# Recurrent layer of a bidirectional encoder: TensorE's order written out by hand, small products grouped, recurrence and within-chunk products given new places in two periods

## The chip, the cores and the metric

The kernel runs on one core of one Trainium2 chip. The metric is the device time of one launch in microseconds (us); the time before is the median of three runs, 2247.12 us (2247.01 to 2252.69).

## The reference

Two residual layers over 256 tokens of width 2048, and a last RMS norm. Layer 1 (a gated MLP with a spatial gate) is not touched. Layer 0 is an RWKV-7 mixer with 64 heads of 64, scanned in both directions:

```python
z = h @ w_in                                  # 2048 -> r, k, v, gate (4096 each), low-rank dw, da
zs = zs + mu_prev * (shift_prev(zs) - zs) + mu_next * (shift_next(zs) - zs)
for d, rev in ((0, False), (1, True)):
    decay = exp(-exp(-softplus(-(w0[d] + tanh(dw[:, :, d]) @ w_up[d])) - 0.5))
    a_d = sigmoid(a0[d] + da[:, :, d] @ a_up[d])
    k_d = k * (1.0 + (a_d - 1.0) * k_a)
    # S_t = S_{t-1} diag(w_t) + (S_{t-1} a_t) b_t^T + v_t k_t^T ;  y_t = S_t r_t
    y = y + wkv_scan(rh, decay, k_d, vh, -kk, kk * a_d, rev)      # kk: k * k_k, normed per head
    bonus = bonus + sum(rh * k_d * r_k) * vh
out = group_norm(y) * ln_w + ln_b + bonus
return (out * silu(gate)) @ w_out
```

## The kernel before, in words

Products in fp32 precision are made of three products of halves: each weight tile is loaded to `raw` (SP's queue, two buffers), ScalarE (ACT) rounds it to its high half `whi`, VectorE (DVE) subtracts to get the low half `wlo`, and `mm3` issues high x high, low x high, high x low on TensorE (PE). A weight tile has four of 16 rows of blocks: `whi_wv7_12` is the last quarter of block 7's v weights.

The 64 heads are worked in 16 blocks of 4 heads (NB = 16). A loop over periods p = 0 to 17 pipelines them. In period p `mains` makes the wide projections of 128x256 (`acck`, `accr` of block p, `accv`, `accg` of block p-1: 384 matmuls); `factors(p)` makes decays and scaled keys (`hs_k`, `hb_k`: sums over heads; `up`: low-rank products into the bank "pf"; `TH`, `TA`: their tanh; `AR`, `BK`: scaled factors); `before(p-1)` makes the within-chunk products `gp` (grams; masked into `Gs` by DVE) for both directions d and then `inverses` (`Dt`, `NQ`: copies of Gs by ACT; `La`, a chain of 31 pairs of DVE steps on `X` and `TD`; `Tn`, `qp`); `transposed_factors` makes `bp` and `BT`; `after(p-2)` makes `values` (`vp`, copied into `SUV` by ACT, and `RC`), the recurrence over four chunks i (`chain`: `xp`, copied to `Xs`; `uu`, copied to `SUV`; `sp`, from which DVE makes the next state `SJ` and ACT copies it to `SUV`; `yp`), and `finish` (group norm, `bb`, `yt`, output). In names, gp7_011 is block 7, half of the heads 0, direction 1, column tile 1; xp6_1 is block 6, chunk 1.

Each of these is a generator that yields times t within a period of 78; a small loop runs whichever is due next. That gives the order in which instructions are emitted. A scheduler then sets the order of every engine's queue with a timeline of its own, in which the emitted order is the priority; an instruction that would wait in this timeline is passed by others. Semaphores between engines follow the final order, and each queue executes strictly in it.

Of the kernel before, what the change touches and what calls it, by code (L numbers as in the profile page):

```python
# [22 lines left out]
def trunk(tc, x, norm_g, final_norm_g, w_in, mu_prev, mu_next, w0, w_up, a0, a_up, k_k, k_a, r_k,  # L23
# [438 lines left out]
    def factors(b, f):  # L462

        cts = (2 * b, 2 * b + 1)
        t0 = 4 * MT + 1
        yield t0
        Kt = f["Kt"]

        SQ = fr.tile([P, 2, T], F32, tag="SS", name=f"SQ{b}")
        for cl in range(2):  # L470
            S.activation(SQ[:, cl], Kt[:, cl], AF.Square, scale=nkkc[:, cts[cl]:cts[cl] + 1])
# [1 line left out]
        n2 = fr.tile([P, TT, 4], F32, tag="n2", name=f"n2_{b}")
        V.tensor_scalar(n2, head_sums(SQ, f"hs_k{b}"), 1e-24, None, ALU.max)
        rn = fr.tile([P, TT, 4], F32, tag="rn", name=f"rn{b}")
        G.tensor_tensor(rn.rearrange("p a b -> p (a b)"), n2.rearrange("p a b -> p (a b)"), halfpow, ALU.pow)
        yield t0 + 8
        rnb = head_bcast(rn, f"hb_k{b}", "pf", 1, fr.tile([P, TT, 4, 64], F32, tag="SS", name=f"exk{b}"))
        yield t0 + 12
        NK = fr.tile([P, 2, T], F32, tag="NK", name=f"NK{b}")  # L480
# [4 lines left out]
        AR = sc.tile([P, 2, 2, NC, 2, C], F32, tag="AR", name=f"AR{b}", bufs=2)  # L485
        yield TUP
        _, wh, wl = f["wu"]
        ups = []
# [73 lines left out]
        f.update(PA=PA, AR=AR, BK=BK, BQ=BQ)  # L562

    def grams(b, f):

# [1 line left out]
        Gs = sc.tile([P, 2, 16, 2 * C], F32, tag="Gs", name=f"Gs{b}", bufs=2)
        for d in range(2):
            for cl in range(2):

                gp = [sm(f"gp{b}_{h}{d}{cl}").rearrange("p (c q t) -> p c q t", c=NC, q=2) for h in range(2)]
                for c in range(NC):
                    for h in range(2):
                        PE.matmul(gp[h][:, c].rearrange("p q t -> p (q t)"),  # L574
                                  BK[H[h], d, cl, c].rearrange("p q t -> p (q t)"),
                                  AR[H[h], d, cl, c].rearrange("p q t -> p (q t)"), start=True, stop=True)
                u0 = (d * 2 + cl) * NC
                for h in range(2):
                    V.tensor_tensor(Gs[:, h, u0:u0 + NC], gp[h].rearrange("p c q t -> p c (q t)"),
                                    gmask[:, d].rearrange("p q t -> p (q t)").unsqueeze(1).to_broadcast([P, NC, 2 * C]),  # L580
                                    ALU.mult)
                yield 4 * (d * 2 + cl + 1)
        f["Gs"] = Gs

# [14 lines left out]
    def inverses(b, f):  # L599
# [8 lines left out]
        for h in range(2):  # L608
# [3 lines left out]
            S.copy(NQ[h * 64:h * 64 + 32], Gs[0:32, h, :, 32:64])  # L612
# [10 lines left out]
        for j in range(31, 0, -1):  # L623
            yield TSUB - (TSUB - 21) * j / 31
            m, n = j // 2, 16 - j // 2
            tv = TD[:, :j * n].rearrange("p (s t) -> p s t", t=n)
            V.tensor_tensor(tv, La[:, j, 0:j].unsqueeze(2).to_broadcast([P, j, n]),  # L627
                            X[:, j:j + 1, m:].to_broadcast([P, j, n]), ALU.mult)
            V.tensor_tensor(X[:, 0:j, m:], X[:, 0:j, m:], tv, ALU.add)  # L629
# [24 lines left out]
    def values(b, f):  # L654

        Vt = f["Vt"]
        SUV = sc.tile([P, 2, 2, NC, 2, C], F32, tag="SUV", name=f"SUV{b}")
        G.memset(SUV[H[0], :, :, 0].rearrange("p d l h v -> p (d l) (h v)"), 0.0)
        vp = sm(f"vp{b}", "pq", 1).rearrange("p (m n) -> p m n", n=P)
        yield 4  # L660
        for cl in range(2):
            for tt in range(TT):
                PE.transpose(vp[:, cl * TT + tt], Vt[:, cl, tt * P:(tt + 1) * P], ident)
        for d in range(2):

            rows_ = SUV[H[1], d].rearrange("p l c h n -> p (l c) (h n)")
            if d == 1:
                rows_ = rows_[:, ::-1]
            for half in range(2):
                S.copy(rows_[:, half::2], vp[H[half]])  # L670
        for h in range(2):
            S.copy(RC[H[0], h], f["AR"][H[h], :, :, :, 1].rearrange("p d l c t -> p (d l c) t"))
# [487 lines left out]
```

## Time and profile before

| | |
|---|---|
| median of three runs | 2247.12 us |
| profiled execution, its own time | 2250.88 us |
| its span | 2249.2 us, mean granted TensorE clock 0.991 |
| busy: PE, PEld, DVE, ACT, POOL | 98%, 87%, 72%, 63%, 8% |
| periods 0 to 5 (from the first `acck` to that of block 6) | 37.9 to 473.4 us |
| periods 6 to 15 | 473.4 to 1265.7 us |
| periods 16 and 17 and the rest of layer 0 | from 1265.7 us |
| layer 1 and the end | about 1430 to 2249 us |

Span is the time from the first to the last instruction; busy time counts an engine's instructions and not its waits. A busy TensorE can still be slowed by what stands next to what in its queue, which shows in the distance of starts and not in the busy share.

### The profile page before, as it was taken

How to read it: one execution, taken by the hardware profiler on the slowest of the kernel's cores; microseconds unless marked ns; L12 is line 12 of the kernel's file. 1: busy time of each engine (PE TensorE's matmuls, PEld its weight loads, DVE VectorE, ACT ScalarE, POOL GpSimd, SP SyncE). 2: the span in 40 equal slices, each digit the busy share in tenths (PEclk: the TensorE clock that was granted, in tenths of full speed). 3: DMA queues.
4: the chain of work that ended last, by engine and by line, in shares of the span. 5: the costliest groups of instructions: out<-in, count | busy, mean ns of one | idle time of the engine just before them, and what ended most of it. 6: DMA issues, size and time to landing. Idle time of an engine off the chain costs nothing.

```text
span 2249.2 us, 48589 instructions
## 1 busy us (share of the span) xinstructions
PE 2200.9 (98%) x19984; PEld 1959.1 (87%) x19984; DVE 1611.2 (72%) x3121; ACT 1406.3 (63%) x2192; POOL 181.0 (8%) x230
## 2 busy tenths in 40 slices
PE   7999999999999999999999999999999999999998
PEld 7898899999999999999999977778888888888886
DVE  5787789778877977877887774465546777777444
ACT  6657777777767777776777864455444444444443
POOL 2210101001011101101010000000000000000000
PEclk9999899999999999999999999999999999999999
DMA  5444244343343343334434455586776666666664
GB/s 169 132 129 132 69 116 116 105 119 114 113 126 109 111 116 119 115 112 125 118 102 125 128 174 175 186 259 189 207 221 192 194 195 193 194 192 194 196 195 156
DMA packets 286127, 339.23 MB, mean 151 GB/s; under 512 B 11600, under 2 KB 233552, under 8 KB 285776
## 3 DMA queue, kind: packets, MB, share of 16 engines
q1 hardware_dynamic: 265648, 314.88, 46.4%
q10 hardware_dynamic: 20256, 21.24, 3.2%
q8 instruction: 157, 2.57, 0.5%
q14 instruction: 66, 0.54, 0.1%
HBM read 329.78 MB, written 6.29 MB: 149 GB/s over the span
## 4 chain that ended last, share of the span: by engine, by line
PE 76%; ACT 10%; DMA 6%; DVE 5%; issue 3%; POOL 0%; ACTq 0%; POOLq 0%; SPq 0%; DVEq 0%
PE uacc L200 5%; PE gacc L200 5%; PE oacc L162 4%; PE oacc L161 4%; PE oacc L163 4%; PE gp L574 4%; PE gacc L202 3%; PE uacc L202 3%; PE vacc L161 3%; PE vacc L162 3%; PE vacc L163 3%; PE accv L161 3%; PE accg L161 2%; PE accg L163 2%; PE accg L162 2%
## 5 line engine op out<-in xcount | busy, mean ns | idle before, releaser
L200 PE MATMUL uacc<-z,whi_u 128*128 128x512 f32 x512 | 179.0, 394 | 0.0
L200 PE MATMUL gacc<-z,whi_g 128*128 128x512 f32 x512 | 177.3, 393 | 0.0
L161 PE MATMUL accv<-zh,whi_wv 128*128 128x256 f32 x512 | 153.9, 301 | 2.3 <-ACT whi_wv L146 2.3
L163 PE MATMUL accg<-zh,wlo_wg 128*128 128x256 f32 x512 | 151.3, 295 | 0.5 <-DVE wlo_wg L147 0.5
L161 PE MATMUL acck<-zh,whi_wk 128*128 128x256 f32 x512 | 150.3, 294 | 1.1 <-ACT whi_wk L146 1.1
L163 PE MATMUL acck<-zh,wlo_wk 128*128 128x256 f32 x512 | 148.6, 290 | 2.7 <-DVE wlo_wk L147 2.7
L163 PE MATMUL accv<-zh,wlo_wv 128*128 128x256 f32 x512 | 149.7, 292 | 1.6 <-DVE wlo_wv L147 1.5
L163 PE MATMUL accr<-zh,wlo_wr 128*128 128x256 f32 x512 | 149.3, 292 | 0.5 <-DVE wlo_wr L147 0.4
L162 PE MATMUL accr<-zl,whi_wr 128*128 128x256 f32 x512 | 148.5, 290 | 0.0
L161 PE MATMUL accr<-zh,whi_wr 128*128 128x256 f32 x512 | 148.3, 290 | 0.0
L161 PE MATMUL accg<-zh,whi_wg 128*128 128x256 f32 x512 | 148.0, 289 | 0.0
L162 PE MATMUL accv<-zl,whi_wv 128*128 128x256 f32 x512 | 147.6, 288 | 0.0
L162 PE MATMUL acck<-zl,whi_wk 128*128 128x256 f32 x512 | 147.3, 288 | 0.0
L162 PE MATMUL accg<-zl,whi_wg 128*128 128x256 f32 x512 | 146.4, 286 | 0.0
L202 PE MATMUL uacc<-z,wlo_u 128*128 128x256 f32 x512 | 142.4, 284 | 0.0
L202 PE MATMUL gacc<-z,wlo_g 128*128 128x256 f32 x512 | 140.2, 279 | 0.0
L147 DVE TENSOR_TENSOR wlo_v<-raw_v,whi_v 128x1024 fp32r<-128x1024 f32 x64 | 78.4, 1225 | 80.3 <-ACT whi_v L146 80.3
L627 DVE TENSOR_TENSOR TD<-La,X 128x126 f32<-128x126 f32 (+22 forms) x496 | 126.7, 255 | 10.5
L629 DVE TENSOR_TENSOR X<-X,TD 128x126 f32<-128x126 f32 (+22 forms) x496 | 125.0, 252 | 9.4
L147 DVE TENSOR_TENSOR wlo_o<-raw_o,whi_o 128x1024 fp32r<-128x1024 f32 x64 | 78.0, 1223 | 74.6 <-ACT whi_o L146 74.3
L147 DVE TENSOR_TENSOR wlo_p<-raw_p,whi_p 128x1024 fp32r<-128x1024 f32 x60 | 73.9, 1232 | 75.6 <-ACT whi_p L146 75.6
L146 ACT CAST whi_p<-raw_p 128x1024 fp32r<-128x1024 f32 x60 | 63.1, 1051 | 91.5 <-PE oacc L163 87.3
(333 smaller groups left out, 6946.9 us busy)
## 6 DMA issues: line engine op xcount, KB each, us to landing
raw_wk<-in_rwkv_w_in_dram SPq DMA_DIRECT2D x64, 512.0 KB, 3.8
raw_wr<-in_rwkv_w_in_dram SPq DMA_DIRECT2D x64, 512.0 KB, 3.7
raw_wv<-in_rwkv_w_in_dram SPq DMA_DIRECT2D x64, 512.0 KB, 3.8
raw_wg<-in_rwkv_w_in_dram SPq DMA_DIRECT2D x64, 512.0 KB, 3.7
raw_o<-in_rwkv_w_out_dram SPq DMA_DIRECT2D x64, 512.0 KB, 4.0
raw_v<-in_gmlp_w_in_dram SPq DMA_DIRECT2D x64, 512.0 KB, 3.7
raw_u<-in_gmlp_w_in_dram SPq DMA_DIRECT2D x64, 512.0 KB, 3.5
raw_g<-in_gmlp_w_in_dram SPq DMA_DIRECT2D x64, 512.0 KB, 3.5
```

The costliest lines, as they stand in the source:

```text
L146: latest[0] = S.copy(hi, raw)
L147: latest[1] = V.tensor_tensor(lo, raw, hi.bitcast(F32), ALU.subtract)
L161: PE.matmul(acc, a[0], b[0], start=first, stop=False, skip_group_check=True)
L162: PE.matmul(acc, a[0], b[1], start=False, stop=False, skip_group_check=True)
L163: PE.matmul(acc, a[1], b[0], start=False, stop=last, skip_group_check=True)
L200: PE.matmul(acc.rearrange("p h t -> p (h t)"), hi[:, j, cs], zc[:, k].rearrange("p h t -> p (h t)"), start=k == 0, stop=False, skip_group_ ...
L202: PE.matmul(acc[:, 0], lo[:, j, cs], zc[:, k, 0], start=False, stop=k == KT - 1, skip_group_check=True)
L574: PE.matmul(gp[h][:, c].rearrange("p q t -> p (q t)"), BK[H[h], d, cl, c].rearrange("p q t -> p (q t)"), AR[H[h], d, cl, c].rearrange("p q ...
L627: V.tensor_tensor(tv, La[:, j, 0:j].unsqueeze(2).to_broadcast([P, j, n]), X[:, j:j + 1, m:].to_broadcast([P, j, n]), ALU.mult)
L629: V.tensor_tensor(X[:, 0:j, m:], X[:, 0:j, m:], tv, ALU.add)
```

## The change

TensorE's queue in the loop over periods is no longer ordered by the scheduler: it executes in the emitted order (`tc.manual_schedule(engines={PE})`). The other engines' queues are still ordered by the scheduler. The emission times are set anew:

- the recurrence starts at 2 (before: 9) with a distance of 13 between chunks (11), `uu` and `sp` 3.5 and 7.6 after `xp` (3.0 and 5.9);
- grams of direction 0 are made at 59.1 and 66.1 in the period of their factors, those of direction 1 at 2.1 and 5.6 in the next one (all four: 0 to 12 of the next period);
- the inverse's steps are spread from 8 to 44 (18 to 50), its products `qp` stand at 59 and 66 (53 and 55);
- `values` moves from 4 in period p to 72 in period p-1;
- the low-rank products leave `factors` for `rates`, at 40, 43, 46, 50 (43 and on, 2 apart); `hs_k` stands at 28.8 (22.5), `hb_k` at 35 (28.5); the factors' steps move by some units;
- `yt` stands at 66 (60), and `OT` has a buffer of its own.

The core of the diff:

```diff
-    PERIOD, CT, TSUB, TBT, TEO, TUP = 78.0, 11.0, 50.0, 36.0, 1.2, 43.0
+    PERIOD, CT, TBT, TEO = 78.0, 13.0, 37.0, 1.2
+    TCH, CB, TUP = 2.0, (3.5, 7.6), (40.0, 43.0, 46.0, 50.0)
+    TGP, TSUB, TQ, TYT = ((59.1, 66.1), (TCH + 0.1, TCH + CB[0] + 0.1)), (8.0, 44.0), (59.05, 66.0), 66.05
...
+    def rates(b, f):
+        f["ups"] = [[], []]
+        for d in range(2):
...
+            for wi, (dst, hb) in enumerate(((th, hw0), (ta, ha0))):
+                yield TUP[2 * d + wi]
+                up = sm(f"up{b}_{d}_{wi}", "pf", 1).rearrange("p (c t) -> p c t", c=2)
...
-        yield t0 + 2
+        yield 28.8
         n2 = fr.tile([P, TT, 4], F32, tag="n2", name=f"n2_{b}")
...
-    def grams(b, f):
+    def grams(b, f, d):
...
+        for cl in range(2):
+            yield TGP[d][cl]
             gp = [sm(f"gp{b}_{h}{d}{cl}").rearrange("p (c q t) -> p c q t", c=NC, q=2) for h in range(2)]
...
+    def early_grams(b, f):
+        yield TGP[0][0]
+        yield from grams(b, f, 0)
...
-            yield TSUB - (TSUB - 21) * j / 31
+            yield TSUB[1] - (TSUB[1] - TSUB[0] - 2) * j / 31
...
     def values(b, f):
+        yield 72
...
-            t = 9 + CT * i
+            t = TCH + CT * i
...
-        OT = sc.tile([P, 2, T], F32, tag="vy", name=f"OT{b}", bufs=2)
+        OT = sc.tile([P, 2, T], F32, tag="OT", name=f"OT{b}")
...
     def before(b, f):
-        yield from grams(b, f)
+        yield from grams(b, f, 1)
         yield from inverses(b, f)
     def after(b, f):
-        yield from values(b, f)
         yield from chain(b, f)
...
+    fixed = tc.manual_schedule(engines={mybir.EngineType.PE})
+    fixed.__enter__()
     for p in range(NB + 2):
...
-            act.append(factors(p, st[p]))
+            act += [rates(p, st[p]), factors(p, st[p]), early_grams(p, st[p])]
         if 0 < p <= NB:
-            act += [before(p - 1, st[p - 1]), transposed_factors(p - 1, st[p - 1])]
+            act += [before(p - 1, st[p - 1]), values(p - 1, st[p - 1]), transposed_factors(p - 1, st[p - 1])]
...
+    fixed.__exit__(None, None, None)
```

In period 0 the emitted order also puts all four `up` and the first two pairs of grams of block 0 ahead of block 1's `acck`.

What moves is seen best at three places of period 8. First TensorE where chunk 0 of block 6's recurrence begins (`xp6_0`), beside block 8's k projection (`acck8`) and the grams of block 7. The queue before:

```order
L163 MATMUL acck8_8396<-zh_187,wlo_wk8_4_8363 128x256
L574 MATMUL gp7_110_8498<-AR7_7755,BK7_8114 128x128
L574 MATMUL gp7_010_8497<-AR7_7755,BK7_8114 128x128
L574 MATMUL gp7_110_8498<-AR7_7755,BK7_8114 128x128
L161 MATMUL acck8_8396<-zh_187,whi_wk8_8_8399 128x256
L162 MATMUL acck8_8396<-zl_188,whi_wk8_8_8399 128x256
L701 MATMUL xp6_0_8521<-SUV6_8428,Gs6_7311 64x64 x2
L163 MATMUL acck8_8396<-zh_187,wlo_wk8_8_8400 128x256
L161 MATMUL acck8_8396<-zh_187,whi_wk8_8_8399 128x256
L162 MATMUL acck8_8396<-zl_188,whi_wk8_8_8399 128x256
L163 MATMUL acck8_8396<-zh_187,wlo_wk8_8_8400 128x256
L701 MATMUL xp6_0_8521<-SUV6_8428,Gs6_7311 64x64 x6
```

Three of gp7's grams stand in one piece and xp6_0 in two, with one to four wide matmuls between. TensorE's queue at the same xp6_0 after the change (left out are five more grams, alternating the same way):

```order
L167 MATMUL acck8_8436<-zh_187,wlo_wk8_0_8354 128x256
L713 MATMUL xp6_0_8465<-SUV6_8402,Gs6_7120 64x64 x8
L584 MATMUL gp7_010_8476<-AR7_7868,BK7_8081 128x128
L584 MATMUL gp7_110_8477<-AR7_7868,BK7_8081 128x128
...
L584 MATMUL gp7_110_8477<-AR7_7868,BK7_8081 128x128
L165 MATMUL acck8_8436<-zh_187,whi_wk8_0_8353 128x256
```

The grams and xp6_0 stood in pieces of two to six matmuls between wide ones; now xp6_0's eight and the eight grams of one pair stand in one group. The next pair follows `uu6_0` in the same way, 18 wide matmuls later.

Second ACT between the copy of xp6_0 and the copy of the next state into SUV, which xp6_1 on TensorE reads. ACT's queue before:

```order
L706 COPY Xs6_0_8530<-xp6_0_8521 128x256
L611 COPY Dt7_8618<-Gs7_8415 32x16x32 x2
L612 COPY NQ7_8619<-Gs7_8415 32x512
L712 COPY SUV6_8428<-uu6_0_8544 64x4x64 x2
L611 COPY Dt7_8618<-Gs7_8415 32x16x32 x2
L146 CAST whi_wr8_4_8575<-raw_wr8_4_8573 128x1024
L612 COPY NQ7_8619<-Gs7_8415 32x512
L621 COPY Gs7_8415<-AR7_7755 64x16x64
L146 CAST whi_wr8_8_8650<-raw_wr8_8_8648 128x1024
L391 ACTIVATE kt8_8640<-acck8_8396,c0_174 128x256
L621 COPY Gs7_8415<-AR7_7755 64x16x64
L729 COPY SUV6_8428<-SJ6_0_8608 64x4x64 x2
```

ACT's queue between the same two copies after the change:

```order
L718 COPY Xs6_0_8474<-xp6_0_8465 128x256
L150 CAST whi_wk8_12_8496<-raw_wk8_12_8494 128x1024
L724 COPY SUV6_8402<-uu6_0_8512 64x4x64 x2
L623 COPY Dt7_8535<-Gs7_8224 32x16x32 x2
L624 COPY NQ7_8536<-Gs7_8224 32x512
L623 COPY Dt7_8535<-Gs7_8224 32x16x32 x2
L624 COPY NQ7_8536<-Gs7_8224 32x512
L150 CAST whi_wr8_0_8565<-raw_wr8_0_8563 128x1024
L633 COPY Gs7_8224<-AR7_7868 64x16x64
L741 COPY SUV6_8402<-SJ6_0_8592 64x4x64 x2
L633 COPY Gs7_8224<-AR7_7868 64x16x64
L150 CAST whi_wr8_4_8624<-raw_wr8_4_8622 128x1024
```

The same copies of Gs stand there, but uu6_0's copy is ahead of them now, only one cast instead of two and no `kt` stand among them; the state's copy SUV<-SJ6_0 comes after one Gs<-AR and not after two. The grams that they read are made right behind uu6_0 now.

Third DVE near the end of the inverse of block 7, where it makes the low half of the last quarter of the v weights, `wlo_wv7_12`. DVE's queue before:

```order
L627 TENSOR_TENSOR TD7_8639<-La7_8632,X7_8634 128x96
L629 TENSOR_TENSOR X7_8634<-X7_8634,TD7_8639 128x8x12
L627 TENSOR_TENSOR TD7_8639<-La7_8632,X7_8634 128x91
L147 TENSOR_TENSOR wlo_wv7_12_9036<-raw_wv7_12_9033,whi_wv7_12_9035 128x1024
L629 TENSOR_TENSOR X7_8634<-X7_8634,TD7_8639 128x7x13
L627 TENSOR_TENSOR TD7_8639<-La7_8632,X7_8634 128x78
L536 TENSOR_TENSOR TH8_0_9045<-TH8_0_9045,kt8_8640 128x512
L539 SCALAR_TENSOR_TENSOR TA8_0_9046<-TA8_0_9046,NK8_8855 128x512
```

DVE's queue around the same wlo_wv7_12 after the change:

```order
L641 TENSOR_TENSOR X7_8557<-X7_8557,TD7_8562 128x16
L644 STREAM_TRANSPOSE TD7_8562<-X7_8557 128x32x16
L542 TENSOR_TENSOR TH8_0_8455<-TH8_0_8455,kt8_8679 128x512
L645 STREAM_TRANSPOSE Tn7_9089<-TD7_8562 128x512
L545 SCALAR_TENSOR_TENSOR TA8_0_8456<-TA8_0_8456,NK8_8968 128x512
L556 TENSOR_TENSOR BK8_9185<-TH8_0_8455,SS8_0_9126 128x8x64
L754 BN_STATS st6_6_9202<-yp6_8457 128x6 x8
L151 TENSOR_TENSOR wlo_wv7_12_9061<-raw_wv7_12_9058,whi_wv7_12_9060 128x1024
L555 TENSOR_TENSOR BK8_9185<-TA8_0_8456,SS8_0_9126 128x8x64
L755 BN_AGGR mv6_9203<-st6_6_9202 128x2 x8
```

The low half stood among the steps on X; now it comes behind the last of them, both transposes, two of block 8's factors, BK and the group norm's statistics of block 6 (`st6_6`).

More of the change, by code (lines that the diff above doesn't have):

```diff
@@ L460, in mains @@
                 yield 12 * MT + i
[L462 to L471, printed above, removed]
-        yield t0 + 2
[L473 to L480, printed above, removed]
-        for cl in range(2):
-            V.scalar_tensor_tensor(NK[:, cl], Kt[:, cl], nkkc[:, cts[cl]:cts[cl] + 1], rnb[:, cl], ALU.mult, ALU.mult)
-        PA = sc.tile([P, NC, 2, 2], F32, tag="PA", name=f"PA{b}", bufs=3)
[L485 to L488, printed above, removed]
+    def rates(b, f):
+        f["ups"] = [[], []]
         for d in range(2):
@@ L498, in factors @@
                 for cl in range(2):
-                    S.activation(dst[:, cl], up[:, cl], AF.Tanh, scale=0.5, bias=hb[d][:, cts[cl]:cts[cl] + 1])
-                yield TUP + 2 * (2 * d + wi + 1)
-            ups.append((th, ta))
+                    S.activation(dst[:, cl], up[:, cl], AF.Tanh, scale=0.5, bias=hb[d][:, 2 * b + cl:2 * b + cl + 1])
+                f["ups"][d].append(dst)
+    def factors(b, f):
+        cts = (2 * b, 2 * b + 1)
+        yield 4 * MT + 1
+        Kt = f["Kt"]
+        SQ = fr.tile([P, 2, T], F32, tag="SS", name=f"SQ{b}")
+        for cl in range(2):
+            S.activation(SQ[:, cl], Kt[:, cl], AF.Square, scale=nkkc[:, cts[cl]:cts[cl] + 1])
+        yield 28.8
+        n2 = fr.tile([P, TT, 4], F32, tag="n2", name=f"n2_{b}")
+        V.tensor_scalar(n2, head_sums(SQ, f"hs_k{b}"), 1e-24, None, ALU.max)
+        rn = fr.tile([P, TT, 4], F32, tag="rn", name=f"rn{b}")
+        G.tensor_tensor(rn.rearrange("p a b -> p (a b)"), n2.rearrange("p a b -> p (a b)"), halfpow, ALU.pow)
+        yield 35
+        rnb = head_bcast(rn, f"hb_k{b}", "pf", 1, fr.tile([P, TT, 4, 64], F32, tag="SS", name=f"exk{b}"))
+        yield 38
+        NK = fr.tile([P, 2, T], F32, tag="NK", name=f"NK{b}")
+        for cl in range(2):
+            V.scalar_tensor_tensor(NK[:, cl], Kt[:, cl], nkkc[:, cts[cl]:cts[cl] + 1], rnb[:, cl], ALU.mult, ALU.mult)
+        PA = sc.tile([P, NC, 2, 2], F32, tag="PA", name=f"PA{b}", bufs=3)
+        AR = sc.tile([P, 2, 2, NC, 2, C], F32, tag="AR", name=f"AR{b}", bufs=2)
+        f.update(PA=PA, AR=AR)
         KD = []
@@ L504, in factors @@
         for d in range(2):
-            t = (TUP + 4, PERIOD * 0.7)[d]
+            t = (46, 55)[d]
             yield t
-            th, ta = ups[d]
+            th, ta = f["ups"][d]
             S.activation(th, th, AF.Identity, bias=1.0)
@@ L536, in factors @@
             eng.tensor_tensor(th, th, Kt, ALU.mult)
-            yield t + 6
+            yield t + 5
             V.scalar_tensor_tensor(ta, ta, 1.0, NK, ALU.add, ALU.mult)
             if d == 0:
-                yield PERIOD * 0.6
+                yield 52
                 BK = se.tile([P, 2, 2, NC, 2, C], F32, tag="BK", name=f"BK{b}")
+                f["BK"] = BK
             def slot(q, natural):
@@ L554, in factors @@
             KD.append(th)
+        yield 67
         eng.tensor_tensor(KD[0], KD[0], KD[1], ALU.add)
-        yield PERIOD * 0.94
+        yield 70
         BQ = fr.tile([P, 2, T], F32, tag="BQ", name=f"BQ{b}", bufs=2)
@@ L561, in factors @@
                                    ALU.mult, ALU.mult)
-        f.update(PA=PA, AR=AR, BK=BK, BQ=BQ)
-    def grams(b, f):
+        f["BQ"] = BQ
+    def grams(b, f, d):
         AR, BK = f["AR"], f["BK"]
[L567 to L577, printed above, removed]
-                for h in range(2):
[L579 to L583, printed above, removed]
+        if d == 0:
+            f["Gs"] = sc.tile([P, 2, 16, 2 * C], F32, tag="Gs", name=f"Gs{b}", bufs=2)
+        Gs = f["Gs"]
+        for cl in range(2):
+            yield TGP[d][cl]
+            gp = [sm(f"gp{b}_{h}{d}{cl}").rearrange("p (c q t) -> p c q t", c=NC, q=2) for h in range(2)]
+            for c in range(NC):
+                for h in range(2):
+                    PE.matmul(gp[h][:, c].rearrange("p q t -> p (q t)"),
+                              BK[H[h], d, cl, c].rearrange("p q t -> p (q t)"),
+                              AR[H[h], d, cl, c].rearrange("p q t -> p (q t)"), start=True, stop=True)
+            u0 = (d * 2 + cl) * NC
+            for h in range(2):
+                V.tensor_tensor(Gs[:, h, u0:u0 + NC], gp[h].rearrange("p c q t -> p c (q t)"),
+                                gmask[:, d].rearrange("p q t -> p (q t)").unsqueeze(1).to_broadcast([P, NC, 2 * C]),
+                                ALU.mult)
+    def early_grams(b, f):
+        yield TGP[0][0]
+        yield from grams(b, f, 0)
     def transposed_factors(b, f):
@@ L643, in inverses @@
             S.copy(NQ[R1[h]], qp[R1[h]])
-        yield TSUB + 5
+        yield TQ[1]
         for u in range(16):
@@ L706, in chain @@
             S.copy(Xs, xp)
-            yield t + CT * 0.27
+            yield t + CB[0]
             up = part("uu", i)
@@ L733, in finish @@
     def finish(b, f):
-        tf = 9 + CT * 3.9
+        tf = TCH + CT * 4 - 1
         yield tf
```

16 lines of the change are left out of this document (8 added, 8 removed).

## The prediction

> **What bounds the kernel now.** I began with the page's first two parts (TensorE 98% busy, granted clock near full), then cut the span into stages by the start of each block's k projection. Columns: stage, its length, busy time (and instructions) of PE, PEld, DVE, ACT, POOL, granted clock, DMA share, GB/s.
>
> ```profile
> PE 2200.9 (98%) x19984; PEld 1959.1 (87%) x19984; DVE 1611.2 (72%) x3121; ACT 1406.3 (63%) x2192; POOL 181.0 (8%) x230
> ...
> 37.90:64.70 26.80, 24.67 (x202) 24.05 (x200) 16.07 (x25) 17.14 (x32) 3.20 (x8) 1.00 0.55 154
> 64.70:473.40 408.70, 395.97 (x4483) 369.56 (x4483) 335.45 (x743) 294.75 (x487) 53.71 (x64) 0.96 0.39 112
> 473.40:1265.70 792.30, 784.60 (x9542) 725.24 (x9540) 638.67 (x1501) 592.52 (x1001) 85.65 (x99) 1.00 0.40 116
> 552.60:1186.60 634.00, 627.68 (x7635) 580.18 (x7633) 511.00 (x1201) 473.89 (x801) 68.63 (x80) 1.00 0.40 116
> 1265.70:1430.00 164.30, 160.63 (x1431) 130.15 (x1430) 95.54 (x185) 97.18 (x152) 4.96 (x5) 1.00 0.54 174
> 1430.00:2249.00 819.00, 809.61 (x4145) 685.34 (x4143) 505.49 (x620) 382.02 (x486) 23.16 (x20) 1.00 0.64 198
> ```
>
> Read three things. From 473.4 to 1265.7 ten periods take 79.2 us each and TensorE is the bound: 627.7 of 634 busy. In that stage DVE is busy 81% and ACT 75%, so either can become late if its work is bunched. The first six periods (37.9 to 473.4) take 435.5 us with less work in them, part of it at a lower granted clock (0.96 in the mean, about 33 us at half). The change ends before 1430, so the last 819 us stay.
>
> The waits of PE in the eight periods from 552.6 have one row:
>
> ```profile
> PE hs_k L402 <- ACT SQ L471: 6.3, 8, 1.3
> ```
>
> That is 0.8 us a period. So a steady gain must come out of TensorE's own time: its order. A piece of the timeline, where a recurrence step (xp) and grams (gp) stand among the k projection, shows what the order costs. First column start, second duration; I use the differences of starts.
>
> ```profile
> 639.41 0.28 PE L163 MATMUL acck<-zh,wlo_wk 128*128 128x256 f32 x1
> 639.62 0.71 PE L574 MATMUL gp<-AR,BK 64*128 64x128 f32 x6
> 640.25 0.39 PE L161 MATMUL acck<-zh,whi_wk 128*128 128x256 f32 x1
> 640.48 0.28 PE L162 MATMUL acck<-zl,whi_wk 128*128 128x256 f32 x1
> 640.69 0.34 PE L701 MATMUL xp<-SUV,Gs 128*64 128x64 f32 x4
> 640.95 0.38 PE L163 MATMUL acck<-zh,wlo_wk 128*128 128x256 f32 x1
> 641.17 0.28 PE L161 MATMUL acck<-zh,whi_wk 128*128 128x256 f32 x1
> 641.29 0.28 PE L162 MATMUL acck<-zl,whi_wk 128*128 128x256 f32 x1
> 641.41 0.28 PE L163 MATMUL acck<-zh,wlo_wk 128*128 128x256 f32 x1
> 641.62 0.57 PE L701 MATMUL xp<-SUV,Gs 128*64 128x64 f32 x12
> 642.12 0.39 PE L161 MATMUL acck<-zh,whi_wk 128*128 128x256 f32 x1
> 642.34 0.28 PE L162 MATMUL acck<-zl,whi_wk 128*128 128x256 f32 x1
> ```
>
> Wide after wide is 0.12 (641.29 to 641.41). The last wide before a small group takes 0.21 (641.41 to 641.62), the first after it 0.22 (642.12 to 642.34). Each trip from wide to small and back thus costs 0.19 us, plus about 0.1 inside the group until its pipeline fills: xp in 4 + 12 records takes 0.26 + 0.50, where its 16 together would take 0.1 + 16 x 0.032 = 0.62.
>
> **The change, part by part.**
>
> *TensorE's price of a steady period.* I priced the static order of one period (block 9's k projection to block 10's) with start-to-start times as above, group by group. The 384 wide matmuls cost 46.1 in both. Before, the small work stands in 72 alternating runs, of which gp 9, recurrence and outputs 15, wide 30; after, 55 runs, with gp 4, recurrence 13, wide 24. The sums: transitions of wide matmuls 4.5 to 3.4; gp 5.8 to 4.4 (6 records cost 0.63 above, and a pair of records alone costs 0.4; 16 whole by the same pitch about 1.1); the low-rank up 3.3 to 2.9; everything else 17.9 to 17.5. In all 77.6 to 74.3, which is -3.3. Measured 79.2 is 77.6, the 0.8 of the hs_k wait, and 0.8 that I can't place. hs_k is emitted at 28.8 instead of some 22, later than the SQ it waits for, so I take its wait to nothing; of the 0.8 I keep half. Without new waits a period would be 74.3 + 0.4 = 74.7: -4.5 a period.
>
> *New waits on a fixed order.* TensorE can no longer be given other work where an operand is late: everything behind it waits. I walked the three other queues by their orders, with these durations (columns: count, busy, mean ns, idle before):
>
> ```profile
> L611 ACT COPY Dt<-Gs 32x512 f32<-32x512 f32 x32 | 34.4, 1074 | 16.9 <-DVE Gs L579 16.6
> L146 ACT CAST whi_wr<-raw_wr 128x1024 fp32r<-128x1024 f32 x32 | 33.5, 1047 | 35.8 <-DMA raw_wr<-in_rwkv_w_in_dram 30.8 <-PE xp L701 4.5
> L729 ACT COPY SUV<-SJ 64x256 f32<-64x256 f32 x48 | 19.4, 404 | 4.0 <-DVE SJ L727 3.3
> L621 ACT COPY Gs<-AR 64x1024 f32<-64x1024 f32 x16 | 16.8, 1051 | 0.4
> L670 ACT COPY SUV<-vp 64x512 f32<-64x512 f32 x32 | 18.5, 579 | 4.0 <-PE vp L663 3.7
> L672 ACT COPY RC<-AR 64x1024 f32<-64x1024 f32 x16 | 16.8, 1050 | 0.1
> L612 ACT COPY NQ<-Gs 32x512 f32<-32x512 f32 x16 | 9.9, 619 | 0.4
> L579 DVE TENSOR_TENSOR Gs<-gp,gmask 128x512 f32<-128x512 f32 x64 | 41.2, 685 | 7.0 <-PE gp L574 7.0
> ```
>
> First, the second recurrence step. xp1 needs the copy SUV<-SJ0, and in ACT's new order this stands behind the copies that now follow the d=1 grams at once. From the start of the last grams: grams about 1.0 until the first half can be read, Gs 0.7, then on ACT Dt twice 2.15, NQ 0.62, the same again 2.77, one cast 1.05, Gs<-AR 1.05, SUV twice 0.81: 10.1 us. TensorE needs xp1 after those grams 1.1, 18 wide 2.35, sp and yp 1.13, 30 wide 3.8: 8.4 us. Wait 1.7. If the scheduler's queue on ACT is entered later than I assume, it is more; the floor is 0, if the Gs come half a step sooner.
>
> Second, the up products share one bank, and the third waits until ACT has read the second (into TA). From the end of the first up ACT has, by the same view, three BT, TH, rt and TH again (3.6), Xs 0.3, RC twice 2.1, Et 0.6, a cast 1.05 and the read 0.8: 8.5 us. TensorE has 7.6 of priced work between: 0.9 of wait, between 0 and 2.
>
> Third, the fourth quarter of the v projection waits for wlo_wv_12, the low half of its weights, which DVE's new order puts behind the whole inverse, its two transposes, BK and the group norm's statistics. From La to its end DVE has 62 inverse steps, 9 low halves, 8 token-shift operations and 25 others.
>
> ```profile
> L627 DVE TENSOR_TENSOR TD<-La,X 128x126 f32<-128x126 f32 (+22 forms) x496 | 126.7, 255 | 10.5
> L629 DVE TENSOR_TENSOR X<-X,TD 128x126 f32<-128x126 f32 (+22 forms) x496 | 125.0, 252 | 9.4
> ...
> L147 DVE TENSOR_TENSOR wlo_wv<-raw_wv,whi_wv 128x1024 fp32r<-128x1024 f32 x32 | 39.2, 1224 | 3.4 <-ACT whi_wv L146 2.4
> ...
> 660.72 1.22 DVE L147 TENSOR_TENSOR wlo_wu<-raw_wu,whi_wu 96x1024 fp32r<-96x1024 f32 x1
> 661.86 0.47 DVE L394 SCALAR_TENSOR_TENSOR kt<-acck,pc,kt 128x255 f32<-128x255 f32 x1
> ```
>
> By durations that is 31 x 0.255 + 31 x 0.252 + 9 x 1.22 + about 16 = 42.8; independent neighbours overlap by some 0.08 (660.72 + 1.22 against 661.86), so by starts 39.9. La starts 6.7 us after the last grams, and DVE's own waits on ACT add 1.5 to 3.5 as in the idle columns: wlo_wv_12 is ready at 48 to 50. TensorE, by price, asks for it at 45.3 to 45.8 plus the first two waits (2.5): about 48. So 0 to 2.5 more; I take 0.9. The three waits lie on one chain of ACT and DVE, so an early one shortens a later one: their sum is between 2.5 and 5, I take 3.4. In ACT's queue nothing that TensorE needs sooner stands behind the waits; SP's weight loads follow the low halves by two buffers and are late only with them.
>
> A steady period is then 74.7 + 3.4 = 78.1, and 79.2 - 78.1 = 1.1, in ten periods -11.
>
> *Start and first periods.* In period 0 the four up products and the first two pairs of grams now stand ahead of the second block's k projection. Before, that projection filled 64.7 to 80.8 between them:
>
> ```profile
> L574 PE MATMUL gp<-AR,BK x80: 272/272/419, 80.8 to 134.5; 64*128 64x128 f32 x80
> ...
> 69.31 0.29 PE L161 MATMUL up<-LTh,whi_wu 96*128 96x256 f32 x1
> ```
>
> The first gram came 11.5 us after the first up. Now TensorE sits idle through most of that: acck1 starts near 80 instead of 64.7, with 4 x 0.7 + 2 x 1.1 of later work done early; a loss of 10 (bounds: 0, if the chain of DVE and ACT goes that much faster undisturbed, and 15.3). Against it, periods 1 to 5 cost 408.7 where the price of before's order is 369; after, the price is 59.8 + 4 x 74.3 = 357. I give them 3.8 of waits each and another 10 in period 1, where the low halves also stand late: 386, -23. Half-clock stretches there, 33 us of them before at a loss of some 16, I take as halved inside this figure and add 6 for what the longer idle in period 0 starts. Together -23 + 10 + 6 = -7.
>
> *Tail, 1265.7 to 1430.* Runs fall from 82 to 58 (about -4), but bp, uu14_3, yp14 and xp15_0 now stand directly behind what they need: 2.7 for xp15_0's copies (four of 0.58 and the step to them) and about 1 each for the others, +5. I take +1.
>
> *Costs of nothing.* OT's own buffer and the split of factors and grams into several generators add no instruction; DVE and ACT do the same count of work. Values moved a few us earlier are hidden under the wide matmuls around them: the vp copies (four of 0.58 on ACT) end about 1.7 us before xp0 asks. If that cover is gone, each period pays the difference.
>
> Sum: -11 - 7 + 1 = -17 against the profiled execution's 2250.9, which ran 3.8 above the median of the runs shown (2247.1). So 2230 on the median's scale.
>
> **The clock.** A wait has a second price. Idle stretches and the granted clock behind them:
>
> ```profile
> 249.80:253.21 3.41, 1.34 (x10) 1.13 (x9) 3.41 (x7) 1.81 (x5) 3.32 (x3) 1.00 0.48 128
> 253.21:270.28 17.07, 16.28 (x109) 15.36 (x110) 12.03 (x25) 14.41 (x25) 1.99 (x2) 0.50 0.27 83
> 137.14:140.55 3.41, 1.68 (x14) 1.48 (x13) 3.41 (x4) 1.54 (x2) 3.41 (x2) 1.00 0.01 4
> 140.55:143.97 3.42, 3.42 (x18) 3.36 (x16) 3.42 (x7) 0.79 (x1) 0.07 (x1) 0.50 0.52 153
> 1304.40:1307.80 3.40, 2.29 (x21) 1.44 (x20) 3.24 (x6) 1.91 (x5) 0.00 (x0) 1.00 0.21 58
> ```
>
> Idle of 2.07 and of 1.73 in 3.41 us were followed by half clock, for 17.1 and 3.4 us; 1.1 was not. xp1's 1.7 is at that edge. A drop of 3.4 us costs 1.7, but TensorE then reaches the later two waits 1.7 later, and those shrink by as much, so I add nothing. The Trainium skill, "TensorE: Matmul & The Clock Gate", Part 1, lets the clock fall only after a whole idle window of about 3.4 us; by that rule waits of 1.7 never cost clock and the slower rival below would fall away. The rows above disagree: windows with 1.3 and 1.7 us of work were followed by half clock, so I keep the rival.
>
> **The rivals.**
> 1. *No new wait of size* (the walks assume that ACT and DVE run in their written order at the durations of before, and may enter each stretch earlier). Then 74.7 a period: -45 in ten periods, -15 to -20 before and in the tail: 2185. For it: DVE and ACT have 15 and 20 us free per period. Against it: the 1.7 at xp1 is a sum of eight rows with one reading.
> 2. *Change of no size.* The waits take 4.5 a period, all that the grouping saves, because TensorE is handed to the chain of ACT and DVE: 79.2 a period, the start as above: 2240 to 2250.
> 3. *Slower, by the clock.* The wait at xp1 exceeds 1.7, the clock halves in every period for more than one stretch, and the loss isn't absorbed, since half-speed grams and recurrence delay ACT and DVE too. Price 74.7 + 5 + 1.7 to 3.4 = 81.4 to 83.1 a period: +22 to +39 in ten, with nothing won at the start: 2265 to 2285. It decides where idle in a 3.41 us window passes about 1.7. For it: the two drops above. Against it: windows with 1.1 us of idle have no drop behind them, and a wait that falls across two windows is halved.
> 4. *The order isn't what costs.* The transitions saved could be hidden by weight loads. Against it: the rows at 641.41 and 642.12; I leave it 3 in 100, inside rival 2.
>
> **How the numbers follow.** Forecast (2210 to 2242) 0.50; rival 1 0.17; rival 2 with 4 0.15; rival 3 0.18. Measured runs of this kernel tell 0.3% (7 us) from no change: faster is under 2240, slower over 2254. Faster is rival 1 and nearly all of the forecast, 0.17 + 0.46 = 0.63; same takes the forecast's last 0.04 and most of rival 2, 0.18; slower 0.19. The range from 2188 to 2262 leaves out half of rival 1 and most of rival 3.
>
> **What would show it.** Right: steady periods of 77 to 79 us; no gp rows in pieces; waits of PE for xp<-ACT SUV of 1.2 to 2 in each period, for up<-ACT TA under 1, for accv<-DVE wlo_wv up to 2.5; acck1 at 77 to 81. Rival 1: none of these over 0.5 and periods near 75. Rival 3: stretches at clock 0.50 after 473. Wrong altogether: a wait that I did not walk, such as bb, qp or hb_k, or weights that come late from SP; then the period's excess over 74.7 has another name.

## The result: slower by 1.1%, and the profile after

The changed kernel takes 2275.9 us (median of 4, 2275.0 to 2276.15) against 2248.2: a ratio of 1.0113 [1.0099, 1.0126]. The forecast was 2230, in a range from 2188 to 2262. The profiled execution of the changed kernel has a span of 2274.2 us, 25.0 more than before.

The stages of the changed kernel, in the columns of the prediction's first fence (period 0, period 1, periods 2 to 5, periods 6 to 15, and what follows, cut where the last `yt` and the first layer-1 projection stand):

```profile
37.40:85.70 48.30, 37.24 (x262) 34.41 (x260) 33.59 (x48) 31.35 (x57) 12.27 (x16) 0.81 0.45 129
85.70:174.70 89.00, 67.10 (x634) 64.46 (x634) 59.67 (x122) 45.09 (x67) 17.08 (x15) 0.83 0.31 88
174.70:486.50 311.80, 300.89 (x3819) 282.49 (x3818) 257.12 (x600) 233.14 (x399) 29.91 (x40) 0.99 0.41 116
486.50:1272.30 785.80, 758.76 (x9542) 711.87 (x9542) 644.68 (x1502) 586.39 (x1001) 74.58 (x99) 0.98 0.41 118
1272.30:1431.20 158.90, 145.25 (x1354) 119.39 (x1352) 85.84 (x174) 88.08 (x141) 5.20 (x5) 0.92 0.49 154
1431.20:1542.00 110.80, 106.18 (x464) 82.19 (x461) 60.64 (x67) 52.84 (x72) 0.00 (x0) 1.00 0.66 216
1542.00:2274.20 732.20, 724.08 (x3739) 616.90 (x3737) 452.05 (x561) 337.27 (x421) 23.18 (x20) 1.00 0.63 193
```

Against before: periods 0 and 1 took 26.8 + 72.7 = 99.5 and take 137.3 (+37.8); periods 2 to 5 took 336.0 and take 311.8 (-24.2); 6 to 15 792.3 and 785.8 (-6.5). The same two pieces of the tail before are these, so the tail gave +18.5: it reached its last `yt` 7.3 sooner and then took 25.8 longer.

```profile
1265.70:1431.90 166.20, 162.53 (x1466) 131.62 (x1464) 96.77 (x186) 97.69 (x152) 4.96 (x5) 1.00 0.54 175
1431.90:1516.90 85.00, 83.66 (x378) 66.89 (x373) 51.08 (x59) 44.40 (x64) 0.00 (x0) 1.00 0.72 232
```

The grouping did its work. On the timeline of the changed kernel in a steady period, xp takes 0.61 and one whole group of grams 1.09, as priced:

```profile
646.26 0.28 PE L167 MATMUL acck<-zh,wlo_wk 128*128 128x256 f32 x1
646.47 0.69 PE L713 MATMUL xp<-SUV,Gs 128*64 128x64 f32 x16
647.08 1.16 PE L584 MATMUL gp<-AR,BK 64*128 64x128 f32 x16
648.17 0.39 PE L165 MATMUL acck<-zh,whi_wk 128*128 128x256 f32 x1
```

What took most of it back are waits (columns: total us, times, longest). Periods 6 to 15, then the largest of periods 0 and 1, then the four largest from 1272.3 to 1350:

```profile
PE xp L713 <- ACT SUV L741: 15.5, 11, 1.6
PE accv L167 <- DVE wlo_wv L151: 5.9, 10, 0.6
PE up L165 <- ACT TA L481: 4.5, 10, 0.5
...
PE qp L653 <- DVE Tn L645: 17.0, 1, 17.0
...
PE bp L606 <- ACT BT L607: 3.0, 1, 3.0
PE xp L713 <- ACT SUV L682: 2.8, 3, 1.6
PE vp L675 <- ACT TTs L662: 2.7, 1, 2.7
PE xp L713 <- ACT SUV L741: 2.3, 1, 2.3
```

The first three are the ones that the prediction had named. The 17.0 is one standstill in period 1, and the last four stand in periods 16 and 17.

The clock shows in two steady periods that wait for the same three things, 1.5, 0.6 and 0.4 us in each, and in the standstill:

```profile
644.20:723.10 78.90, 76.22 (x956) 71.58 (x955) 64.11 (x151) 58.27 (x100) 7.46 (x10) 0.98 0.40 117
958.70:1036.10 77.40, 74.71 (x956) 70.12 (x955) 64.25 (x151) 58.50 (x100) 7.48 (x10) 1.00 0.42 119
139.60:156.60 17.00, 0.02 (x2) 0.02 (x2) 16.20 (x38) 2.95 (x6) 3.46 (x4) 0.50 0.30 89
```

The first has one 3.4 us stretch of half clock behind xp's wait, the second none: 1.5 us of difference. Seven of the ten periods from 486.5 have such a stretch. The trace's clock records show what divides them. All stretches of half clock in this execution begin and end on marks 3.41 us apart, the first period's at 661.64 and 665.06:

```profile
658.23:661.64 3.41, 1.76 (x18) 1.42 (x17) 3.03 (x7) 3.36 (x6) 0.00 (x0) 1.00 0.01 2
661.64:665.06 3.42, 3.42 (x38) 3.30 (x37) 2.90 (x9) 2.14 (x3) 0.00 (x0) 0.50 0.50 153
```

In the seven periods xp's wait begins 0.5 to 1.3 us behind such a mark, in the other three 1.7 to 1.9 us behind one. Why the place counts, no run varied.

### The profile page after: what moved, and what is told of

Its sections match the earlier page's. It is cut to its first block, busy times and chain, and to the rows that moved or that the text cites. A ratio compares the mean times of both kernels' runs of the same rounds, so it can differ in the third digit from the quotient of the medians.

```text
span 2274.2 us, 48533 instructions
## 1 busy us (share of the span) xinstructions
PE 2164.4 (95%) x19984; PEld 1936.0 (85%) x19984; DVE 1613.6 (71%) x3121; ACT 1396.5 (61%) x2192; POOL 172.5 (8%) x230
## 4 chain that ended last, share of the span: by engine, by line
PE 67%; DVE 12%; ACT 11%; DMA 6%; issue 4%; POOL 1%; ACTq 0%; POOLq 0%; SPq 0%; DVEq 0%
PE uacc L204 5%; PE gacc L204 5%; PE oacc L165 4%; PE oacc L166 4%; PE oacc L167 4%; PE accr L165 3%; PE gacc L206 3%; PE uacc L206 3%; PE vacc L167 3%; PE gp L584 3%; PE vacc L165 3%; PE vacc L166 3%; PE accg L165 2%; PE accr L166 2%; PE accr L167 2%
## 5 line engine op out<-in xcount | busy, mean ns | idle before, releaser
L165 PE MATMUL accr<-zh,whi_wr 128*128 128x256 f32 x512 | 156.4, 305 | 0.8 <-ACT whi_wr L150 0.8
L165 PE MATMUL acck<-zh,whi_wk 128*128 128x256 f32 x512 | 155.9, 304 | 0.1
L165 PE MATMUL accg<-zh,whi_wg 128*128 128x256 f32 x512 | 155.7, 304 | 0.0
L167 PE MATMUL accg<-zh,wlo_wg 128*128 128x256 f32 x512 | 145.1, 283 | 2.0 <-DVE wlo_wg L151 2.0
L151 DVE TENSOR_TENSOR wlo_v<-raw_v,whi_v 128x1024 fp32r<-128x1024 f32 x64 | 78.4, 1225 | 80.4 <-ACT whi_v L150 80.4
L151 DVE TENSOR_TENSOR wlo_p<-raw_p,whi_p 128x1024 fp32r<-128x1024 f32 x60 | 73.9, 1231 | 75.7 <-ACT whi_p L150 75.7
L151 DVE TENSOR_TENSOR wlo_wk<-raw_wk,whi_wk 128x1024 fp32r<-128x1024 f32 x64 | 78.2, 1222 | 63.2 <-ACT whi_wk L150 60.9
```

The lines of the kernel that those rows point to most:

```text
L151: latest[1] = V.tensor_tensor(lo, raw, hi.bitcast(F32), ALU.subtract)
L165: PE.matmul(acc, a[0], b[0], start=first, stop=False, skip_group_check=True)
L167: PE.matmul(acc, a[1], b[0], start=False, stop=last, skip_group_check=True)
```

## The experiments

Durations by stage come from each kernel's own profiled execution. The time of the kernel before, run beside them, was 2248 to 2251.

**Fixed order in periods 2 to 15 alone.**

```diff
-    fixed = tc.manual_schedule(engines={mybir.EngineType.PE})
-    fixed.__enter__()
     for p in range(NB + 2):
+        if p == 2:
+            fixed = tc.manual_schedule(engines={mybir.EngineType.PE})
+            fixed.__enter__()
+        if p == NB:
+            fixed.__exit__(None, None, None)
...
-    fixed.__exit__(None, None, None)
```

> TensorE's order is fixed only in periods 2 to 15; in periods 0, 1, 16 and 17 the scheduler orders it, with the new emission times. Theory A (a fixed order costs where a period has less TensorE work than its timetable of 78, at both ends, because nothing later can fill the waits): periods 0 and 1 together go from 137 us back to about 100, the stretch from period 16 on from 1002 to about 985, steady periods stay at 77.5 to 79; total 2276 - 37 - 17 = 2222 (2215 to 2232). Rival B (the new emission times cost the ends, whoever orders): periods 0 and 1 stay above 125 and the total above 2260.

Measured 2252.4, ratio to before 1.0016 [1.0006, 1.0026]; expected 2222. By stage (periods 0 and 1, period 2, from 16 on), and period 2's largest wait:

```profile
38.10:137.20 99.10, 93.17 (x746) 89.54 (x745) 77.72 (x121) 68.00 (x111) 23.10 (x28) 0.97 0.45 136
137.20:249.50 112.30, 87.76 (x1105) 81.47 (x1104) 83.51 (x200) 66.03 (x112) 11.98 (x14) 0.85 0.29 87
...
1270.80:2255.70 984.90, 969.02 (x5548) 812.89 (x5546) 598.04 (x801) 477.65 (x633) 28.69 (x25) 1.00 0.62 193
...
PE qp L653 <- DVE Tn L645: 14.2, 1, 14.2
```

The tail came out as expected (984.9, -17.0) and so did periods 0 and 1 (99.1). But period 2 took 112.3 instead of 77.6, with the standstill of qp in it: periods 0 to 2 together 211.4, after the change 214.9. Half of theory A fell: the loss isn't tied to the two first periods.

**New times, no fixed order** (the three `fixed` lines taken out).

> The new emission times with the scheduler ordering TensorE throughout. Theory A: the ends are as before the change (periods 0 and 1 near 100, from period 16 on near 985), small groups are broken up again (70 runs a period instead of 55), no xp wait of 1.5, steady periods 78 to 79; total 2238 to 2252. Rival B: ends as slow as after the change, total above 2270.

Measured 2239.4, 0.9951 [0.9932, 0.997], as expected. In the free order TensorE runs ahead with wide work in the first periods and puts other work off; here it has made that up only by the end of period 8, so the stages are cut at the start of period 9 and of period 16, where the number of matmuls done is the same as after the change. Periods 0 to 8, 9 to 15 and the rest, then the first two stages before the change and after it:

```profile
37.60:706.50 668.90, 647.17 (x7572) 604.88 (x7571) 543.53 (x1220) 491.46 (x824) 78.95 (x101) 0.98 0.39 117
706.50:1252.50 546.00, 541.89 (x6681) 504.32 (x6680) 451.05 (x1052) 413.06 (x702) 73.23 (x69) 1.00 0.40 119
1252.50:2233.80 981.30, 968.15 (x5548) 813.40 (x5546) 597.81 (x801) 476.04 (x630) 28.71 (x25) 1.00 0.62 193
...
37.90:711.00 673.10, 656.10 (x7547) 611.23 (x7545) 543.24 (x1218) 489.92 (x819) 88.31 (x101) 0.97 0.40 115
711.00:1265.70 554.70, 549.13 (x6680) 507.62 (x6678) 446.95 (x1051) 414.49 (x701) 54.26 (x69) 1.00 0.40 116
...
37.40:723.10 685.70, 633.76 (x7572) 595.91 (x7571) 543.47 (x1220) 485.11 (x821) 81.62 (x100) 0.96 0.40 113
723.10:1272.30 549.20, 530.23 (x6681) 497.32 (x6680) 451.60 (x1052) 410.86 (x702) 52.22 (x69) 0.99 0.41 118
```

The new times alone make the kernel faster, and mostly in the steady part: a period there takes 78.0 instead of 79.2. The order fixed on top of them gains in no stage. For the same matmuls it takes 16.8 us more up to period 9, 3.2 more in periods 9 to 15 (about what single runs of one kernel differ by) and 20.6 more behind them. So the new times alone win as much in the steady part as the changed kernel does; what the grouping saves there, its waits and slow stretches take back.

**Old times, fixed order.** The kernel before, with `manual_schedule` around the loop and nothing else.

> The kernel before with nothing changed but TensorE's order fixed as emitted, old emission times. The price of its steady period by the same rows is 74.6 in 55 runs, so the grouping comes from the fixing alone. Theory A: the old times put operands closer to their producers, so waits of 4 to 8 us a period appear (xp, qp, hs_k, accv) and periods cost 79.5 to 83; both ends lose as after the change; total 2290 to 2350. Rival D (the new times bring nothing over the old ones): total within 2270 to 2282.

Measured 2431.3, 1.081 [1.0786, 1.0833]: the direction was right, the size far off. Steady periods cost 89.5. Their price is 74.6, as low as that of the changed kernel, so the small price comes from the fixing. The new times are what keeps the waits of a fixed order small, so rival D is out. Stage and waits of ten periods:

```profile
522.90:1417.60 894.70, 812.32 (x9543) 752.62 (x9541) 654.25 (x1502) 596.95 (x1003) 79.86 (x99) 0.94 0.34 103
...
PE hs_k L402 <- ACT SQ L471: 32.5, 20, 1.8
PE xp L701 <- ACT SUV L729: 23.5, 10, 2.4
PE up L161 <- ACT TA L499: 20.8, 10, 2.1
```

That is 7.7 us a period in these three, 8.0 in all, at the top of the expected 4 to 8; what I had left out is the clock at 0.94: 11.6 us of half clock a period by the clock records, or 5.8 of loss.

**Chunks 1 to 3 three units later.**

```diff
-            t = TCH + CT * i
+            t = TCH + CT * i + (3 if i else 0)
```

> Recurrence chunks 1 to 3 are emitted 3 units later, some 14 wide matmuls more between sp of chunk 0 and xp of chunk 1; DVE's order comes out with wlo_wv_12 ahead of the transposes. Theory A (the xp wait is ACT's queue, a fixed delay that wide matmuls can cover; the clock drops follow from it): the 1.55 us wait for SUV is gone, so is the granted clock of 0.5 after period 2, steady periods 75.0 to 75.8, total about 2276 - 14 x 3.1 = 2232. Rival C (the three waits are one chain of ACT and DVE; what xp no longer waits, up and accv wait): xp's wait is gone but up and wlo_wv together wait 2.5 or more, periods stay at 77 to 78, total above 2258.

Measured 2233.6, 0.9933 [0.9909, 0.9956]; expected 2232. Periods 6 to 15 and the rest, and the two largest waits of periods 6 to 15:

```profile
476.30:1230.00 753.70, 743.94 (x9543) 700.52 (x9542) 643.38 (x1502) 590.19 (x1002) 89.91 (x99) 1.00 0.41 123
1230.00:2229.50 999.50, 974.68 (x5547) 818.82 (x5546) 598.26 (x801) 478.89 (x633) 28.13 (x25) 0.99 0.61 190
...
PE accg L167 <- DVE wlo_wg L151: 6.0, 10, 0.6
PE xp L713 <- ACT SUV L741: 0.7, 3, 0.3
```

Periods of 75.4, no half clock between 163 and 1275 us, and 0.8 us of waits a period. But the scheduler had also reordered DVE and ACT here (`wlo_wv_12` ahead of the transposes, the copies `kt` and `SQ` earlier), so this run doesn't tell whether xp's delay alone was covered.

**Chunks 1 to 3 one unit later.** The same line with 1 in place of 3. `wlo_wv_12` comes out still further back in DVE's queue: behind the transposes and the statistics, as in the changed kernel, and also behind a second BK and the eight BN_AGGR that follow it (`mv`).

> Chunks 1 to 3 of the recurrence 1 unit later instead of 3; DVE's order keeps wlo_wv_12 behind the transposes and the statistics. Separate delays: xp waits 0.7 to 1.0 instead of 1.55, up and accv wait what they did (0.45, 0.57), no stretch of half clock after period 2, steady periods 76.4 to 76.9, total 2246 to 2254. One chain (rival C): xp waits less but up and accv wait that much more (1.6 or more together), periods stay at 77.2 to 77.6, without half clock: total 2257 to 2264.

Measured 2304.8, 1.0229 [1.0196, 1.0262], outside both; steady periods took 79 to 82, in part at half clock. The waits of ten periods:

```profile
PE hs_k L406 <- ACT SQ L492: 19.5, 10, 2.2
PE up L165 <- ACT TA L481: 9.4, 10, 0.9
PE accv L167 <- DVE wlo_wv L151: 8.8, 10, 1.8
PE xp L713 <- ACT SUV L741: 8.4, 10, 0.8
```

xp waits 0.84 instead of 1.55, as both said. up and accv together wait 1.82 instead of 1.04, which fits rival C (1.6 or more), but accv's part can as well come from the new place of its low half on DVE. And hs_k, at its old time but now ahead of xp of chunk 2, waits 1.95, which neither theory had.

**The same, with hs_k behind that xp.**

```diff
-        yield 28.8
+        yield 30.6
```

> The kernel with chunks 1 to 3 one unit later, and hs_k back behind the next xp (emitted at 30.6). ACT's order stays, DVE's order has wlo_wv_12 one step earlier (ahead of the statistics, 1.04 us). If hs_k's wait of 2.0 us is only its place ahead of the copy SQ: it goes, periods without half clock fall from 79.1 to 77.0 to 77.4, total 2305 - 28 = 2270 to 2282. One chain (rival C): up and accv take it back, periods stay at 78.5 or more, total above 2290.

Measured 2259.7, 1.0051 [1.0037, 1.0065]. Steady periods fell from 79 to 82 to 77.1, as expected if the wait is its place alone, and the total by more than I said, because the half clock went too. Ten periods:

```profile
PE xp L713 <- ACT SUV L741: 14.1, 20, 1.9
PE up L165 <- ACT TA L481: 9.5, 10, 1.0
```

hs_k waits no more. Nor does accv, whose low half stands ahead of the statistics on DVE here. But xp now waits at chunk 2 too, 0.57 more, and up still waits 0.95. The sum of waits is 2.4, near the 2.6 of the changed kernel, in other places. Rival C's periods of 78.5 or more did not come.

**Fixed in periods 5 to 15, three units.** As the first experiment, with `p == 5`, and the line with 3.

> Chunks 1 to 3 of the recurrence 3 units later, and TensorE's order fixed in periods 5 to 15 alone. Theory A2 (the start's loss is the wait for block 0's inverse in the first full period that is fixed; the scheduler lets TensorE run ahead by a period and works that lead off by period 5): no wait of qp over 3, periods 0 to 5 together near 430 us instead of 449, periods 6 to 15 at 75.2 each, from period 16 on near 983 instead of 1002: total 2200 to 2212. Rival E (any change from free to fixed order pays some 14 us, wherever it is made): a wait of 10 to 17 us for qp in period 5, total 2215 to 2228.

Measured 2223.4, 0.9873 [0.9857, 0.989], above theory A2's range and inside rival E's, but without the long wait for qp that rival E stands on. Period 5:

```profile
382.90:482.00 99.10, 92.26 (x1227) 85.40 (x1226) 79.92 (x199) 73.96 (x131) 13.32 (x17) 0.91 0.29 88
...
PE xp L713 <- ACT yn L781: 3.1, 1, 3.1
PE qp L653 <- DVE Tn L645: 2.2, 1, 2.2
```

It holds 1227 matmuls, where a period after it holds about 956: the free order had put the others off. qp waits 2.2 us; in four places together the waits are 6.6 us, and 17.1 us run at half clock. Without both the period would take 84.0 (99.1 - 6.6 - 8.5).

**Three units, free from period 16 on** (`fixed.__exit__` at `p == NB`).

> Chunks 1 to 3 three units later, TensorE's order fixed in periods 0 to 15, free from 16 on. The tail theory alone: the start as in the kernel with 3 units (439 us), steady 75.2, from period 16 on 983 instead of 999.5: total 2233.6 - 16.5 = 2217 (2211 to 2222).

Measured 2217.4, 0.9859 [0.9839, 0.9879]; expected 2217. The tail:

```profile
1229.50:2212.90 983.40, 967.83 (x5536) 812.95 (x5534) 596.49 (x800) 476.09 (x631) 28.65 (x25) 1.00 0.62 193
```

Nothing but the tail's order differs from the run with 3 units, whose tail took 999.5.

**The same, with block 0's qp behind period 1's wide matmuls.**

```diff
...
+    def products(b, f, tq=TQ):
...
-            act += [before(p - 1, st[p - 1]), values(p - 1, st[p - 1]), transposed_factors(p - 1, st[p - 1])]
+            act += [before(p - 1, st[p - 1]), values(p - 1, st[p - 1]), later(transposed_factors(p - 1, st[p - 1]), 8.0 if p == 2 else 0.0)]
         if p > 1:
-            act.append(after(p - 2, st[p - 2]))
+            act.append(after(p - 2, st[p - 2]) if p > 2 else later(after(0, st[0]), 6.0))
+        if p == 2:
+            act.append(products(0, st[0], (0.5, 5.0)))
...
```

`products` holds qp and the copies to TTs, taken out of `inverses`; `later` adds its second argument to the emission times.

> As the one before, and block 0's products qp moved from period 1 to the first 5 units of period 2, behind the rest of period 1's wide matmuls and 12 of block 2's; block 0's recurrence 6 units and block 1's bp 8 units later in period 2. Theory F (in period 1 the fixed order holds some 18 us of ready wide matmuls behind qp, which waits for the inverse): the 17 us wait falls under 4 and most of the 24 us of half clock with it, period 1 at 70 to 74 instead of 89, period 2 at 77 to 80 instead of 75: total 2196 to 2206. Rival E2 (the lag is that of the whole chain of DVE and ACT, and comes back in period 2): periods 1 and 2 together stay above 158, total above 2210.

Measured 2218.0, 0.987 [0.9845, 0.9895]: no gain over the one before. Periods 1 and 2, and period 2's largest wait:

```profile
85.20:156.40 71.20, 62.42 (x505) 59.75 (x505) 54.01 (x105) 39.60 (x58) 16.24 (x13) 0.96 0.37 109
156.40:251.80 95.40, 82.86 (x1085) 77.49 (x1085) 68.66 (x166) 65.05 (x110) 9.21 (x12) 0.93 0.32 97
...
PE qp L660 <- DVE Tn L645: 6.2, 1, 6.2
```

Period 1 fell to 71.2, as theory F had it, and period 2 rose to 95.4: together 166.6, with the qp in period 1 163.0. qp still waits 6.2 us. Rival E2 holds: the lag is not one badly placed instruction.

## Why the prediction was wrong, by its steps

**TensorE's price and the waits in a steady period** held. Price and rest were put at 74.7; the changed kernel's shortest period without half clock is 77.4, less 2.6 of waits 74.8 (the other two without it take 77.8 and 78.4). The waits were xp 1.55 (put at 1.7), up 0.45 (0.9), accv 0.59 (0.9), 2.6 in sum against 3.4, on the lower edge of the range. On the timeline of the period from 644.2 xp asks 8.4 us after the start of the last grams, as put, and starts 9.9 us after it (put at 10.1). That the three waits are one chain is shown in part only: in both runs with 1 unit up waits 0.95 instead of 0.45, where xp of chunk 1 waits 0.7 less; for accv it isn't shown, since its low half stood in another place of DVE's queue in both. And the prediction set its gain against the order of before. With the new times the free order is better too: 78.0 a period in periods 9 to 15, where the fixed one takes 78.5.

**The clock** is a step that failed. I added nothing for it, since later waits would shrink by what a slow stretch costs. They don't: the two periods shown above have the same waits, and the one with the slow stretch is 1.5 longer. Seven stretches cost some 10.5 us. That the ten periods still gave 6.5 of the forecast 11 is luck, since the waits came out smaller than put by 0.8 a period, some 8 us. The Trainium skill, "TensorE: Matmul & The Clock Gate", Part 1, lets the clock fall after a whole idle window of about 3.4 us. The trace doesn't agree: seven times a slow stretch stands behind a wait of 1.55. Three times none does, and by the marks shown above the place of the wait divides them. The run with the order fixed in periods 2 to 15 shows the same: in its periods 6 to 15, eight waits that begin up to 1.4 us behind a mark are followed by half clock, two that begin 1.5 and 1.7 us behind one are not. Where no steady wait passes 0.6 (three units) there is no slow stretch.

**The tail** is the second step that failed: +18.5 where I had +1. I had counted single waits, about 5 us, and set savings against them. The idle time of TensorE up to the last `yt` is 13.7 us (158.9 less 145.3) against 3.7 before, and 24 us run at half clock, 12 of loss, for which I had put nothing. Before, the scheduler put output-projection matmuls into such gaps: 422 were done by 1431 us, now 336; the other 86, at 0.23 each, are 20 of the 25.8 us by which the next piece is longer. That the fixed order does it is shown twice: with that order free from period 16 on, all else the same, the stretch takes 983.4 instead of 999.5; and 984.9 instead of 1001.9 where periods 0 and 1 are free as well.

**The start** is the third and largest: I had periods 0 to 5 at -7, and they gave +13.6. Periods 2 to 5 were right (311.8; 4 x 78.1 = 312). Period 0 was put at 10 more and 6 for the clock, and lost 21.5: acck1 started at 85.7 instead of 80, with 18 us of half clock ahead of it. Period 1 was put at 73.6 and took 89.0. The 10 for low halves that "also stand late" had the wrong place: what stood late was the inverse of block 0, on which qp waited 17.0 us with 18.1 us of the period's work behind it. The clock was at half for 24 us around that wait, of which 6.7 us fell on work.

What this loss is, the runs narrow down. It is not the new times: in free order they take 16.8 us less up to period 9, for the same matmuls. It doesn't belong to periods 0 and 1: left free, they take 99.1 and the first fixed one 112.3; left free to period 5, that one takes 99.1 instead of 84.0. Nor does it belong to qp's place. In the free order TensorE runs ahead of block 0's inverse with the next block's projections (before the change period 2 began at 137.4 us, and block 0's qp stood at 177.5) and catches up by degrees: before the change periods 2 to 5 hold 674, 1156, 1055 and 1063 matmuls, and each from 6 on some 956. The emitted order asks that each block's inverse be done when its turn comes, and whichever period it begins in waits until DVE and ACT have made up that lead. That reading fits the four runs, but the lead itself was not varied. In the standstill of 17.0 us DVE was busy for 16.2; which part of its work sets the end stays open.

By stage the forecast misses 4.5 us in periods 6 to 15, 17.5 in the tail and 20.6 at the start. That is 42.6 of the 45.9; most of the rest is the 3.8 that was taken off for the median.

**The rivals.** The time fell into rival 3's, 2265 to 2285, but not by its mechanism. It needed steady periods of 81 to 83, and they are 78.6; its clock loss came at a third to two thirds of the price that I gave (1.0 a period in the mean), and the ends decided.

## What to carry to other kernels

A price for an order, counted in transitions, held to 1.1 us a period in the steady part of two fixed kernels here, once waits and half clock are taken off (74.8 against 74.7, and with the old times 75.7 against 74.6). It says nothing of what the scheduler would make of the same new times, and that was better than the changed kernel here (2239.4 us against 2275.9), so the new times should be tried with the free order first. And a fixed order is only as good as its timetable where work per period is not the steady one: walk the filling and the draining of a pipeline instance by instance, since there the scheduler fills gaps with work of later steps and a fixed order cannot. Each small wait that a fixed order brings should be given more independent work ahead of it, and be followed on every queue, because a shift of one unit can move another product ahead of its operand (hs_k, 2 us a period) while a shift of three, with the orders of DVE and ACT that came with it, clears the waits. The version that came of it here, three units and the tail left free, takes 2217.4 us, 1.4% less than before.
